# Shared projections of a two-layer decoder: a key or query pair's end in four parts with its scaling on ScalarE, tiles loaded a step ahead, and two pairs' forget gates moved to the front

## The chip, the core and the metric

The kernel runs on one core of a Trainium2 chip. A core has TensorE (matrix products; PE in the profile, PEld for its weight loads), VectorE (DVE), ScalarE (ACT), GpSimd (POOL), SyncE (SP, which issues the DMAs here) and 16 DMA engines. Each engine works through its own list of instructions in order and waits on semaphores for the others. The metric is the device time of one execution in microseconds (us).

## The reference, cut to what matters

One gated-DeltaNet layer (8 heads of 128) is followed by one forgetting-attention layer that reads a shared K/V. The change touches mainly the part between them: the projections to keys, queries, values, output gates and forget gates, all of the normalised residual stream `h` (2048 x 1024, float32).

```python
def shared_kv(h, kv_norm, kv_w, kv_forget_bias, kv_k_norm):
    u = rms_norm(h, kv_norm)
    k, v, f = jnp.split(u @ kv_w, [FOX_WIDTH, 2 * FOX_WIDTH], axis=-1)
    k = rms_norm(k.reshape(B, L, FOX_HEADS, HEAD_DIM), kv_k_norm)   # per head of 128
    log_f = jax.nn.log_sigmoid(f + kv_forget_bias)
    c = jnp.cumsum(log_f, axis=1)
    return k, v, c

def fox_mixer(h, k, v, c, w_in, q_norm, w_out):
    q, z = jnp.split(h @ w_in, [FOX_WIDTH], axis=-1)
    q = rms_norm(q.reshape(B, L, FOX_HEADS, HEAD_DIM), q_norm)
    o = fox_attention(q, k, v, c) * jax.nn.silu(z)
    return o @ w_out
```

## The kernel before, in words

The program has four stages: the DeltaNet layer (projections, chunked rule), its output product (class `Wout`), the shared projections (class `Shared`), and attention with its output product. Every product of two float32 matrices is done as three products of rounded halves (`split` writes a high and a low part, `mm3` adds three matmuls).

`Shared` takes the 2048 rows as 8 pairs of 128-row tiles, in three blocks of 2, 3 and 3 pairs (`BLOCKS`). For each block it runs through 8 groups of weight columns, two for each of the kinds k, q, v and z. In a group each 2x2 block product is done in seven products instead of eight (`PRODUCTS`, in the order P1 P6 P7 P5 P2 P4 P3), so a group is seven steps, and a step has 12 matmuls of 128x256 for each pair of the block: 3 pairs make 7*3*12 = 252 matmuls, 2 pairs 168. One pair's 12 matmuls are called a pair-step here.

What feeds and empties them:

- `raw` loads a group's weights (`w`), `sums` (POOL, line 913) forms `T1` to `T3` of the next group and `T4` of this one, `columns` splits them into `gh` (ACT cast, line 124) and `gl` (DVE subtraction, line 125), two products ahead, in three buffers. So a `gh` of a product waits until the product three before it is finished.
- `prep` makes the row operands `hP`, `lP` of a pair: it loads two tiles `ht` of `h_d`, scales them, transposes them on TensorE into `pth` and splits seven combinations. It is a generator; `run` takes its steps at fixed groups of the block before, and for the first block the loop at the end of `tile_yoco` takes them at the places in `ready` while `Wout` runs.
- The results `X` and `Y` of the products are gathered into `cc` by ACT (lines 984, 986) and DVE (line 989).
- `finish` ends a pair after its P3. For keys and queries: squares of the whole `cc` (ACT, line 1035), row sums by head `kss` (DVE, 1037 and 1038), root `krs` (POOL power, line 119), `cc` times `krs` (DVE, line 1041), and then, as two entries of `pend`, two `turn`s: four transposes into `ptr` (TensorE, line 1049), a scaled copy `kt` (ACT, line 1051) and a store. `tick` counts `pend` down once for each pair-step, so the first turn stands five pair-steps after the pair's P3 and the second six.
- `forget_weights` prepares the forget-gate columns `wf` and is called at the start of `run`; `forget` does a pair's gates (32 small matmuls into `pf`, a copy `fT`, two transposes) in the block's group 1.

```python
            ss = q2.tile([P, 8], F32, tag="kss", name="kss" + n)
            nc.vector.tensor_reduce(out=ss, in_=sq, axis=mybir.AxisListType.X, op=ALU.add)
            nc.vector.tensor_scalar(out=ss, in0=ss, scalar1=1.0 / P, scalar2=EPS, op0=ALU.mult, op1=ALU.add)
            rs = q2.tile([P, 8], F32, tag="krs", name="krs" + n)
            rsqrt(k, rs, ss, 8)
            nc.vector.tensor_tensor(out=c8, in0=c8, in1=rs.unsqueeze(2).to_broadcast([P, 8, P]), op=ALU.mult)
```

A scheduler of the language places each engine's instructions by priority and its own estimates, so the order on an engine can differ from the order in which the code names the operations; the orders shown further down are those of the built programs.

In the DeltaNet stage `gain` scales the weights of the shared projections ahead of time: at every third weight tile it loads a tile `wgr`, scales it on ACT (line 205) and stores it to `wg_d`.

## Time and profile before

| | |
|---|---|
| median of three runs | 3067.0 us (3064.26 to 3077.52) |
| the profiled execution | 3070.3 us, of which the program's span is 3068.3 us |
| DeltaNet stage, span 0 to 1186 us | 1186 us |
| rest of `Wout`, 1186 to 1414 us | 228 us |
| shared projections, 1414 to 2318 us | 904 us |
| attention and output, 2318 to 3068 us | 750 us |

Times inside the execution are counted from the span's start. In a row of a timeline stand the start, the duration, the engine, the line, the operation, the tile written and those read, and in brackets how long the engine had been idle before it and what ended that wait. Matmuls overlap, so 12 of 0.28 us that follow one another take about 1.4 us. A `PEclk` of 1.00 means TensorE at its higher level (2.4 GHz) throughout the stretch, 0.50 at its lower level (1.2 GHz).

### The profile page before, as it was taken

The numbers are of one execution on the slowest core, as the hardware profiler recorded it, in microseconds if no ns is written. First come the engines' busy times: TensorE is split into PE (matmuls) and PEld (weight loads), VectorE is DVE, ScalarE is ACT, GpSimd is POOL, SyncE is SP. The second block draws the span as 40 slices with busy tenths as digits, with TensorE's granted clock in tenths as the row PEclk, the third lists the DMA queues.
The fourth block names the chain that finished last, engine by engine and source line by source line (L and its number), as shares of the span: only waits on it lengthen the run. The fifth ranks groups of instructions, "written<-read, shape, count | busy, mean of one in ns | idle before, by whom it ended". The sixth has DMA issues, their size and how long they took to land.

```text
span 3068.3 us, 49714 instructions
## 1 busy us (share of the span) xinstructions
PE 2810.4 (92%) x17910; PEld 2434.8 (79%) x17910; DVE 2051.3 (67%) x5094; ACT 1448.2 (47%) x3288; POOL 991.8 (32%) x810
## 2 busy tenths in 40 slices
PE   7889999999999999988788988988897999999999
PEld 6677778877878787777788888978896888888787
DVE  6777766776777776445668555765557888888522
ACT  5445554454455444343444333433334776776421
POOL 6543111121111111244445233433322444444222
PEclk9999999999999999998888889989898999999999
DMA  6655764475457445343233223322224233332443
GB/s 225 216 183 175 227 192 148 146 252 185 146 176 243 143 135 160 115 153 126 96 124 124 76 80 111 126 76 76 93 95 127 89 94 94 103 94 86 138 144 107
DMA packets 296796, 421.86 MB, mean 137 GB/s; under 512 B 69739, under 2 KB 184678, under 8 KB 295526
## 3 DMA queue, kind: packets, MB, share of 16 engines
q1 hardware_dynamic: 296384, 418.63, 42.1%
q8 instruction: 141, 2.31, 0.3%
q14 instruction: 105, 0.86, 0.1%
q10 hardware_dynamic: 166, 0.06, 0.0%
HBM read 296.92 MB, written 121.70 MB: 136 GB/s over the span
## 4 chain that ended last, share of the span: by engine, by line
PE 52%; DVE 20%; POOL 5%; issue 5%; ACT 4%; DMA 3%; SPq 0%; DVEq 0%; POOLq 0%; ACTq 0%
PE Y L978 9%; PE X L978 5%; DVE acc_q L409 4%; PE pt L1312 3%; POOL krs L119 2%; DVE cc L1041 2%; PE ps L132 2%; PE ppwf L132 2%; PE ppwf L130 2%; PE ppwf L131 2%; PE ps L130 2%; PE ps L131 2%; PE po L132 2%; PE po L131 2%; PE po L130 2%
## 5 line engine op out<-in xcount | busy, mean ns | idle before, releaser
L130 PE MATMUL pp_q<-xh_q,wh_q 128*128 128x512 f32 x768 | 326.8, 425 | 1.5 <-ACT acc_q L407 0.8
L978 PE MATMUL Y<-gh_P,hP 128*128 128x256 f32 x1024 | 302.4, 295 | 14.3 <-DVE cc L989 11.3
L132 PE MATMUL pp_q<-xh_q,wl_q 128*128 128x512 f32 x768 | 308.4, 402 | 0.0
L131 PE MATMUL pp_q<-xl_q,wh_q 128*128 128x512 f32 x768 | 306.4, 399 | 0.0
L978 PE MATMUL Y<-gl_P,hP 128*128 128x256 f32 x1024 | 299.0, 292 | 0.0
L978 PE MATMUL Y<-gh_P,lP 128*128 128x256 f32 x1024 | 297.5, 291 | 0.0
L978 PE MATMUL X<-gh_P,hP 128*128 128x256 f32 x768 | 229.1, 299 | 19.8 <-POOL hrs L119 6.5
L913 POOL TENSOR_TENSOR T<-w,T 128x1024 f32<-128x1024 f32 x48 | 115.1, 2399 | 390.8 <-DVE gl_P L125 380.6
L409 DVE SCALAR_TENSOR_TENSOR acc_q<-cx_q,cols,acc_q 128x512 f32<-128x512 f32 x288 | 226.9, 788 | 13.6 <-ACT acc_q L407 10.5
L978 PE MATMUL X<-gl_P,hP 128*128 128x256 f32 x768 | 225.2, 293 | 8.9 <-DVE gl_P L125 8.9
L978 PE MATMUL X<-gh_P,lP 128*128 128x256 f32 x768 | 225.8, 294 | 2.1 <-DVE lP L125 2.1
L978 PEld LDWEIGHTS Y<-gh_P,hP 128*128 128x128 f32 x1024 | 206.8, 202 | 16.7 <-issue 9.3
L125 DVE TENSOR_TENSOR pl<-pt,ph 128x512 fp32r<-128x512 f32 (+1 forms) x320 | 191.5, 605 | 39.1 <-ACT ph L124 37.3
L124 ACT CAST ph<-pt 128x512 fp32r<-128x512 f32 (+1 forms) x320 | 161.5, 518 | 92.6 <-PE pt L1312 91.7
L978 PEld LDWEIGHTS Y<-gl_P,hP 128*128 128x128 f32 x1024 | 204.8, 200 | 0.0
L978 PEld LDWEIGHTS Y<-gh_P,lP 128*128 128x128 f32 x1024 | 204.5, 200 | 0.0
L1298 ACT ACTIVATE s<-s,nm 128x128 f32<-128x128 f32 (+15 forms) x128 | 154.3, 1206 | 65.9 <-DVE nm L1296 65.7
L412 ACT ACTIVATE th_q<-acc_q 128x512 f32<-128x512 f32 x96 | 60.6, 631 | 251.8 <-DVE acc_q L409 248.5
L1312 PE MATMUL pt<-ident,s 128*128 128x128 f32 x1088 | 172.7, 274 | 2.4 <-DVE pl L125 2.3
L989 DVE TENSOR_TENSOR cc<-cc,Y 128x256 f32<-128x256 f32 x256 | 104.9, 417 | 103.2 <-PE Y L978 102.7
L132 PEld LDWEIGHTS pp_q<-xh_q,wl_q 128*128 128x128 f32 x768 | 146.0, 190 | 34.2
L978 PEld LDWEIGHTS X<-gh_P,hP 128*128 128x128 f32 x768 | 155.9, 203 | 21.2 <-ACT gh_P L124 7.5
(485 smaller groups left out, 8369.3 us busy)
## 6 DMA issues: line engine op xcount, KB each, us to landing
w<-wg_d SPq DMA_DIRECT2D x48, 1024.0 KB, 5.0
wh_q<-w_d SPq DMA_DIRECT2D x72, 512.0 KB, 4.4
wl_q<-w_d SPq DMA_DIRECT2D x72, 512.0 KB, 4.4
wg_d<-wgr SPq DMA_DIRECT2D x32, 512.0 KB, 5.0
w_d<-wh_q SPq DMA_DIRECT2D x24, 512.0 KB, 4.7
w_d<-wl_q SPq DMA_DIRECT2D x24, 512.0 KB, 3.1
wh_q_z<-w_d SPq DMA_DIRECT2D x24, 512.0 KB, 3.5
wl_q_z<-w_d SPq DMA_DIRECT2D x24, 512.0 KB, 4.9
```

What stands on the lines that cost most here:

```text
L119: k.nc.gpsimd.tensor_tensor(out=out, in0=x, in1=k.mhalf[:, :n], op=ALU.pow)
L124: i = k.nc.scalar.copy(hi, src)
L125: (eng or k.nc.vector).tensor_tensor(out=lo, in0=src, in1=f(hi), op=ALU.subtract)
L130: nc.tensor.matmul(out, ah, bh, start=start, stop=False)
L131: nc.tensor.matmul(out, ah, bl, start=False, stop=False)
L132: nc.tensor.matmul(out, al, bh, start=False, stop=stop)
L409: nc.vector.scalar_tensor_tensor(out=acc, in0=cx[:, j:j + TB], scalar=cw[j], in1=acc, op0=ALU.mult, op1=ALU.add)
L913: self.k.nc.gpsimd.tensor_tensor(out=t, in0=a, in1=b, op=ALU.subtract)
L978: nc.tensor.matmul(R, a[:, kt], w[:, kt], start=first and kt + j == 0, stop=last and kt + j == 5, skip_group_check=True)
L989: nc.vector.tensor_tensor(out=dst, in0=src, in1=R, op=ALU.add)
L1298: e = nc.scalar.activation(s[:, 0:w], s[:, 0:w], AF.Exp, bias=nm, accum_out=ls[:, ii:ii + 1])
L1312: nc.tensor.transpose(out=pt[:, ii * P:(ii + 1) * P], in_=Ps[ii][:, j * P:(j + 1) * P], identity=k.ident)
```

## The change

1. A key or query pair's end is cut in four (`squares(0)` in `finish`, `root` one pair-step later, `norm` three after that, the turns one pair-step later than before). The squares and row sums come in two halves of 512 columns. The multiplication by `krs` goes from one DVE instruction of 128x1024 to eight ACT instructions of 128x128, each with its column of `krs` as scale. `cc` has five buffers instead of four, `kss` and `krs` four.
2. The gate kind z is done in two halves too.
3. `prep` loads a tile `ht` one step before its use, and `run` and `ready` step it accordingly (one step more per pair).
4. `forget_weights` is called before `prep` of the first block, with its tiles in other pools; the first block's `forget` runs ahead of all groups, the other blocks' as before.
5. `gain` scales and stores a tile at the call after its load.

```diff
@@ gain
+        if count[0] % 3 == 1 and loaded:
+            i, kt, wr, col = loaded.pop(0)
+            nc.scalar.activation(wr, wr, AF.Copy, scale=k.cols[:, col + kt:col + kt + 1])
+            nc.sync.dma_start(wg_d[i, kt], wr)
...
         nc.sync.dma_start(wr, w[kt * P:(kt + 1) * P, base:base + D])
-        nc.scalar.activation(wr, wr, AF.Copy, scale=k.cols[:, col + kt:col + kt + 1])
-        nc.sync.dma_start(wg_d[i, kt], wr)
+        loaded.append((i, kt, wr, col))
@@ Shared.prep
+        ht = load(2 * p)
+        yield
         for i in range(2):
             tt = 2 * p + i
-            ht = p2.tile([P, D], F32, tag="ht", bufs=1, name=f"ht{tt}")
-            nc.sync.dma_start(ht, h_d[tt * P:(tt + 1) * P, :])
...
                 nc.scalar.copy(q[i, kg], pt)
+                if (i, kg) == (0, 1):
+                    ht = load(2 * p + 1)
                 yield
@@ Shared.run
-        self.forget_weights()
+        gates = [self.forget(*pair) for pair in self.BLOCKS[0]]
+        for x in gates + gates:
+            next(x, None)
...
-                    cc[p] = q2.tile([P, 2, 512], F32, tag="cc", bufs=4, name=f"cc{nm}")
+                    cc[p] = q2.tile([P, 2, 512], F32, tag="cc", bufs=5, name=f"cc{nm}")
...
-            if gi in (1, 3) and pi in (0, 2, 4) and pi // 2 < len(pairs) and gi == 1:
+            if b and gi == 1 and pi in (0, 2, 4):
@@ Shared.finish
-            sq = self.q1.tile([P, 8, P], F32, tag="sq", name="sq" + n)
-            nc.scalar.activation(sq, c8, AF.Square)
-            ss = q2.tile([P, 8], F32, tag="kss", name="kss" + n)
-            nc.vector.tensor_reduce(out=ss, in_=sq, axis=mybir.AxisListType.X, op=ALU.add)
-            nc.vector.tensor_scalar(out=ss, in0=ss, scalar1=1.0 / P, scalar2=EPS, op0=ALU.mult, op1=ALU.add)
-            rs = q2.tile([P, 8], F32, tag="krs", name="krs" + n)
-            rsqrt(k, rs, ss, 8)
-            nc.vector.tensor_tensor(out=c8, in0=c8, in1=rs.unsqueeze(2).to_broadcast([P, 8, P]), op=ALU.mult)
+            def squares(hf):
+                sq = self.q1.tile([P, 4, P], F32, tag="sq", name=f"sq{n}_{hf}")
+                nc.scalar.activation(sq, c8[:, 4 * hf:4 * hf + 4], AF.Square)
+                nc.vector.tensor_reduce(out=ss[:, 4 * hf:4 * hf + 4], in_=sq, axis=mybir.AxisListType.X, op=ALU.add)
+
+            def root():
+                squares(1)
+                nc.vector.tensor_scalar(out=ss, in0=ss, scalar1=1.0 / P, scalar2=EPS, op0=ALU.mult, op1=ALU.add)
+                rsqrt(k, rs, ss, 8)
+
+            def norm():
+                for i in range(8):
+                    nc.scalar.activation(c8[:, i], c8[:, i], AF.Copy, scale=rs[:, i:i + 1])
+
+            squares(0)
+            pend.append([1, root])
+            pend.append([4, norm])
...
-            pend.append([5, lambda: turn(0)])
-            pend.append([6, lambda: turn(1)])
+            pend.append([6, lambda: turn(0)])
+            pend.append([7, lambda: turn(1)])
@@ tile_yoco
     sh = Shared(k, ins, dram, wg_d, sa)
+    sh.forget_weights()
...
-    ready = ready[0:4] + [ready[3] + 8 + 2 * i for i in range(7)] + ready[4:8] + [ready[7] + 8 + 2 * i for i in range(7)]
+    ready = [r for i in (0, 4) for r in [ready[i + 2] - 6] + [ready[i + 2] + 4 * j for j in range(4)]
+             + [ready[i + 2] + 24 + 2 * j for j in range(7)]]
```

ACT at the end of group 10 (a query group of the block with pairs 2, 3 and 4), before. In a name the first number is the group, the next the pair: `sq10_2` is that of pair 2; `gh11_P7` is the cast for product P7 of group 11.

```order
L1035 ACTIVATE sq10_2_19141<-cc10_2_18861 128x1024
L124 CAST gh11_P7_19196<-T11_3_19079 128x1024
L1035 ACTIVATE sq10_3_19162<-cc10_3_18891 128x1024
L984 COPY one11_2_19201<-X11_2_19200 128x256
L984 COPY one11_3_19216<-X11_3_19215 128x256
L984 COPY one11_4_19231<-X11_4_19230 128x256
L1035 ACTIVATE sq10_4_19183<-cc10_4_18921 128x1024
L1051 ACTIVATE kt10_2_0_19250<-ptr10_2_0_19245,qns_98 128x512
L124 CAST gh11_P5_19253<-T11_1_18943 128x1024
L1051 ACTIVATE kt10_2_1_19276<-ptr10_2_1_19271,qns_98 128x512
```

The same place after the change, from the copy `one11_2` to the first copy `kt` (both halves of the first pair's squares and `gh11_P7` stand ahead of it):

```order
L998 COPY one11_2_19354<-X11_2_19353 128x256
L998 COPY one11_3_19374<-X11_3_19373 128x256
L1053 ACTIVATE sq10_4_0_19336<-cc10_4_19057 128x512
L1063 ACTIVATE cc10_2_18997<-cc10_2_18997,krs10_2_19294 128x128 x3
L1053 ACTIVATE sq10_3_1_19339<-cc10_3_19027 128x512
L1063 ACTIVATE cc10_2_18997<-cc10_2_18997,krs10_2_19294 128x128 x3
L1053 ACTIVATE sq10_4_1_19368<-cc10_4_19057 128x512
L1063 ACTIVATE cc10_2_18997<-cc10_2_18997,krs10_2_19294 128x128 x2
L998 COPY one11_4_19397<-X11_4_19396 128x256
L1063 ACTIVATE cc10_3_19027<-cc10_3_19027,krs10_3_19312 128x128 x8
L124 CAST gh11_P5_19419<-T11_1_19087 128x1024
L1077 ACTIVATE kt10_2_0_19442<-ptr10_2_0_19437,qns_98 128x512
```

Between the squares of pairs 3 and 4 now stand the scalings of pair 2, so these squares come behind `krs10_2`; the casts of group 11 from P5 on and the first copy `kt` come behind the scalings of pair 3.

POOL at the same place, before (`T12_3` is the sum T3 of group 12):

```order
L913 TENSOR_TENSOR T11_2_19034<-w11_1_18797,T11_1_18943 128x1024
L913 TENSOR_TENSOR T11_2_19034<-w11_1_18797,T11_2_19034 128x1024
L119 TENSOR_TENSOR krs10_2_19146<-kss10_2_19143,mhalf_76 128x8
L913 TENSOR_TENSOR T12_3_19475<-w12_1_19193,w12_0_19191 128x1024
L119 TENSOR_TENSOR krs10_3_19167<-kss10_3_19164,mhalf_76 128x8
L119 TENSOR_TENSOR krs10_4_19188<-kss10_4_19185,mhalf_76 128x8
L913 TENSOR_TENSOR T12_1_19339<-w12_0_19191 128x1024
```

POOL there after the change:

```order
L925 TENSOR_TENSOR T11_2_19186<-w11_1_18920,T11_2_19186 128x1024
L925 TENSOR_TENSOR T12_3_19657<-w12_1_19346,w12_0_19344 128x1024
L119 TENSOR_TENSOR krs10_2_19294<-kss10_2_19293,mhalf_76 128x8
L119 TENSOR_TENSOR krs10_3_19312<-kss10_3_19311,mhalf_76 128x8
L119 TENSOR_TENSOR krs10_4_19335<-kss10_4_19334,mhalf_76 128x8
L925 TENSOR_TENSOR T12_1_19513<-w12_0_19344 128x1024
L925 TENSOR_TENSOR T12_2_19612<-w12_1_19346,T12_1_19513 128x1024
```

The sum `T12_3` of the next group has moved from behind the first pair's root to ahead of it. On TensorE, at this end of group 10, the transposes `ptr` of all three pairs stood within P6 of group 11 (the last one behind the first matmul of P7); after the change those of the first pair stand within P6, behind 6 pair-steps, those of the second in P7 and those of the third in P5.

TensorE at the start of the shared projections, before (`ppwg_15` is the last product of `Wout`, `X0_0` the first of pair 0):

```order
L130 MATMUL ppwg_15_1_15445<-wgwh7_13653,ohwg_15_15440 128x512
L131 MATMUL ppwg_15_1_15445<-wgwl7_13654,ohwg_15_15440 128x512
L132 MATMUL ppwg_15_1_15445<-wgwh7_13653,olwg_15_15441 128x512
L823 MATMUL pth4_0_15888<-ident_60,ht4_15885 128x128 x4
L978 MATMUL X0_0_15610<-gh0_P1_15576,hP1_0_14688 128x256
L978 MATMUL X0_1_15625<-gh0_P1_15576,hP1_1_14818 128x256
L978 MATMUL X0_0_15610<-gl0_P1_15577,hP1_0_14688 128x256
L978 MATMUL X0_0_15610<-gh0_P1_15576,lP1_0_14689 128x256
```

And after the change (`pf0`, `pf1` are the gates of pairs 0 and 1, 32 matmuls each):

```order
L131 MATMUL ppwg_15_1_15462<-wgwl7_13654,ohwg_15_15457 128x512
L132 MATMUL ppwg_15_1_15462<-wgwh7_13653,olwg_15_15458 128x512
L897 MATMUL pf0_15601<-hP1_0_14708,wf_14637 128x128
L897 MATMUL pf0_15601<-lP1_0_14709,wf_14637 128x128
...
L897 MATMUL pf1_15636<-hP4_1_14914,wf_14637 128x128
L897 MATMUL pf1_15636<-lP4_1_14915,wf_14637 128x128
L904 MATMUL pg0_15671<-ident_60,fT0_15634 128x32 x2
L992 MATMUL X0_0_15692<-gh0_P1_15593,hP1_0_14708 128x256
L992 MATMUL X0_0_15692<-gl0_P1_15594,hP1_0_14708 128x256
L904 MATMUL pg1_15677<-ident_60,fT1_15669 128x32 x2
```

The 64 gate matmuls stand ahead of the first product, and the transposes `pth4` of pair 2 are gone from this place.

## Rows read from the trace of the kernel before

**Rows 1.** The page: span of the profiled execution.

```profile
span 3068.3 us, 49714 instructions
```

**Rows 2.** Shared projections: busy us (xinstructions) of PE, PEld, DVE, ACT, POOL; PEclk; DMA.

```profile
1414.30:2318.00 903.70, 776.59 (x6005) 763.03 (x6003) 562.68 (x722) 344.59 (x484) 347.79 (x158) 0.91 0.29 99
```

**Rows 3.** The same by group: 2 pairs, 3 pairs, 3 pairs of kind v.

```profile
1503.20:1533.30 30.10, 24.59 (x185) 24.08 (x184) 19.08 (x23) 13.08 (x17) 13.80 (x7) 0.89 0.30 105
...
1806.90:1851.40 44.50, 36.94 (x278) 36.38 (x277) 25.79 (x31) 16.11 (x22) 16.02 (x8) 0.88 0.25 84
...
1900.00:1929.50 29.50, 29.27 (x249) 29.10 (x248) 14.41 (x21) 10.80 (x17) 11.61 (x6) 1.00 0.47 161
```

**Rows 4.** Waits of TensorE, 1420 to 2318 us: us, times, longest.

```profile
PE ptr L1049 <- DVE cc L1041: 61.6, 23, 4.5
...
PE ptr L1049 <- DVE kss L1038: 9.8, 4, 3.4
...
PE pth L823 <- DVE fT L888: 5.7, 1, 5.7
```

**Rows 5.** Timeline at the end of group 10: DVE.

```profile
1802.56 1.22 DVE L1037 TENSOR_REDUCE kss<-sq 128x8 f32<-128x1024 f32 x1 [0.61 <-ACT sq L1035]
...
1804.10 1.22 DVE L125 TENSOR_TENSOR gl_P<-T,gh_P 128x1024 fp32r<-128x1024 f32 x1
1806.85 3.36 DVE L1041 TENSOR_TENSOR cc<-cc,krs 128x1024 f32<-128x1024 f32 x1 [1.53 <-POOL krs L119]
```

**Rows 6.** The same stretch: ACT.

```profile
1801.47 1.06 ACT L1035 ACTIVATE sq<-cc 128x1024 f32<-128x1024 f32 x1 [1.68 <-DVE cc L989]
1802.95 1.05 ACT L124 CAST gh_P<-T 128x1024 fp32r<-128x1024 f32 x1 [0.42 <-PE Y L978]
```

**Rows 7.** The same stretch: POOL.

```profile
1804.27 2.54 POOL L119 TENSOR_TENSOR krs<-kss,mhalf 128x8 f32<-128x8 f32 x1 [0.74 <-DVE kss L1038]
1806.78 2.34 POOL L913 TENSOR_TENSOR T<-w,w 128x1024 f32<-128x1024 f32 x1
1811.62 1.64 POOL L119 TENSOR_TENSOR krs<-kss,mhalf 128x8 f32<-128x8 f32 x1 [2.50 <-DVE kss L1038]
```

**Rows 8.** The same stretch: transposes on TensorE.

```profile
1810.35 0.89 PE L1049 MATMUL ptr<-ident,cc 128*128 128x128 f32 x4 [3.18 <-DVE cc L1041]
...
1816.54 0.60 PE L1049 MATMUL ptr<-ident,cc 128*128 128x128 f32 x4
...
1822.20 1.09 PE L1049 MATMUL ptr<-ident,cc 128*128 128x128 f32 x4 [4.12 <-DVE cc L1041]
```

**Rows 9.** Line 1041: times, then ns (least/median/most).

```profile
L1041 DVE TENSOR_TENSOR cc<-cc,krs x32: 1224/3352/3366, 1461.7 to 2198.1; 128x1024 f32<-128x1024 f32 x32
```

**Rows 10.** Timeline: four scalings of 128x128 by a column on ACT.

```profile
646.03 1.14 ACT L431 ACTIVATE kd_q<-pt_q,eg_q 128x128 f32<-128x128 f32 x4 [0.59 <-PE pa_q1g L583]
```

**Rows 11.** Timeline, start of the shared projections: POOL and DVE.

```profile
1426.69 2.34 POOL L913 TENSOR_TENSOR T<-w,T 128x1024 f32<-128x1024 f32 x1 [0.38 <-DMA w<-wg_d]
1427.09 5.08 DVE L869 TENSOR_SCALAR wfz<-wfz,cols 128x8 f32<-128x8 f32 x8 [4.68 <-DMA wfz<-in_kv_w_dram]
...
1432.31 1.22 DVE L125 TENSOR_TENSOR gl_P<-T,gh_P 128x1024 fp32r<-128x1024 f32 x1
```

**Rows 12.** The same stretch: TensorE.

```profile
1421.24 0.77 PE L978 MATMUL X<-gh_P,hP 128*128 128x256 f32 x2 [6.55 <-POOL hrs L119]
...
1430.16 0.58 PE L978 MATMUL X<-gh_P,hP 128*128 128x256 f32 x1 [3.77 <-ACT gh_P L124]
```

**Rows 13.** Timeline of TensorE: transposes of the first block's rows.

```profile
1309.22 1.94 PE L823 MATMUL pth<-ident,ht 128*128 128x128 f32 x8 [4.99 <-issue]
...
1325.62 1.70 PE L823 MATMUL pth<-ident,ht 128*128 128x128 f32 x8 [3.87 <-DVE ht L818]
```

**Rows 14.** Line 205: what ACT waited for before it (us, times).

```profile
  DMA wgr<-in_kv_w_dram: 8.6, 4
  DMA wgr<-in_fox_w_in_dram: 6.0, 4
```

More of the change, by code (lines that the diff above doesn't have):

```diff
@@ L813, in prep, with load @@
         q = {}
+        def load(tt):
+            ht = p2.tile([P, D], F32, tag="ht", bufs=1, name=f"ht{tt}")
+            nc.sync.dma_start(ht, h_d[tt * P:(tt + 1) * P, :])
+            return ht
+        ht = load(2 * p)
+        yield
         for i in range(2):
             tt = 2 * p + i
-            ht = p2.tile([P, D], F32, tag="ht", bufs=1, name=f"ht{tt}")
-            nc.sync.dma_start(ht, h_d[tt * P:(tt + 1) * P, :])
             nc.vector.tensor_scalar(out=ht, in0=ht, scalar1=k.hrs[:, tt:tt + 1], scalar2=None, op0=ALU.mult)
@@ L861, in forget_weights @@
         nc = k.nc
-        self.wf = self.q1.tile([P, 12, P], F32R, name="wf")
-        wz = self.q2.tile([P, 2, 512], F32, tag="cc", bufs=4, name="wfz")
-        nc.gpsimd.memset(wz[:, 0, 0:P], 0.0)
-        nc.gpsimd.tensor_copy(self.wf, wz[:, 0, 0:P].unsqueeze(1).to_broadcast([P, 12, P]))
+        self.wf = self.p1.tile([P, 12, P], F32R, name="wf")
+        wz = self.p2.tile([P, 4, P], F32, tag="s1", name="wfz")
+        nc.gpsimd.memset(wz[:, 0], 0.0)
+        nc.gpsimd.tensor_copy(self.wf, wz[:, 0].unsqueeze(1).to_broadcast([P, 12, P]))
         wr = wz[:, 1, 0:12 * H].rearrange("p (t h) -> p t h", h=H)
@@ L998, in run @@
                         later = [self.prep(*nxt[0], h_d)]
-                    if gi == 1:
-                        next(later[0], None)
-                    if gi == 2:
+                    if gi in (1, 2):
                         next(later[0], None)
@@ L1007, in run @@
                     later = [self.prep(p, s, h_d) for p, s in soon]
-                if gi in (5, 6) and pi < 4:
+                if gi in (5, 6) and pi < 5:
                     next(later[gi - 5])
@@ L1012, in run @@
                         next(x, None)
+                    if pi == 4 and len(later) > 2:
+                        next(later[2])
                     if pi == 6 and len(later) > 2:
@@ L1033, in finish @@
             c8 = flat.rearrange("p (a d) -> p a d", d=P)
-            sq = self.q1.tile([P, 8, P], F32, tag="sq", name="sq" + n)
-            nc.scalar.activation(sq, c8, AF.Square)
-            ss = q2.tile([P, 8], F32, tag="kss", name="kss" + n)
-            nc.vector.tensor_reduce(out=ss, in_=sq, axis=mybir.AxisListType.X, op=ALU.add)
-            nc.vector.tensor_scalar(out=ss, in0=ss, scalar1=1.0 / P, scalar2=EPS, op0=ALU.mult, op1=ALU.add)
-            rs = q2.tile([P, 8], F32, tag="krs", name="krs" + n)
-            rsqrt(k, rs, ss, 8)
-            nc.vector.tensor_tensor(out=c8, in0=c8, in1=rs.unsqueeze(2).to_broadcast([P, 8, P]), op=ALU.mult)
+            ss = q2.tile([P, 8], F32, tag="kss", bufs=4, name="kss" + n)
+            rs = q2.tile([P, 8], F32, tag="krs", bufs=4, name="krs" + n)
+            def squares(hf):
[12 more added lines that the diff above has]
+            pend.append([4, norm])
             gain = k.cols[:, C_KN:C_KN + 1] if kind == "k" else k.qns
@@ L1054, in turn @@
                 nc.sync.dma_start(dst[h0:h0 + 2, :, p * 256:p * 256 + 256].rearrange("h p t -> p h t"), kt_)
-            pend.append([5, lambda: turn(0)])
-            pend.append([6, lambda: turn(1)])
+            pend.append([6, lambda: turn(0)])
+            pend.append([7, lambda: turn(1)])
             return
         if kind == "z":
-            th = self.q1.tile([P, 8, P], F32, tag="sq", name="th" + n).rearrange("p a d -> p (a d)")
-            nc.scalar.activation(th, flat, AF.Tanh, scale=0.5)
-            nc.vector.scalar_tensor_tensor(out=flat, in0=th, scalar=1.0, in1=flat, op0=ALU.add, op1=ALU.mult)
+            for t in range(2):
+                th = self.q1.tile([P, 4, P], F32, tag="sq", name=f"th{n}_{t}").rearrange("p a d -> p (a d)")
+                nc.scalar.activation(th, c[:, t], AF.Tanh, scale=0.5)
+                nc.vector.scalar_tensor_tensor(out=c[:, t], in0=th, scalar=1.0, in1=c[:, t], op0=ALU.add, op1=ALU.mult)
         dst = self.v if kind == "v" else self.z
```

5 lines of the change are left out of this document (3 added, 2 removed).

## Prediction, made before the changed kernel ran

> **What bounds the kernel now.** I read the page first, then busy time by stage, then by group of weight columns, then what TensorE waited for, and last a timeline of one group's end. The span is 3068.3 us [rows 1]; the profiled execution took 3070.3 us, 3.3 above the median of 3067.0. TensorE is the engine that is nearly always busy, and it has the most slack to lose in the shared projections: of 903.7 us it is busy 776.6, and its granted clock is 0.91 [rows 2], so 18% of the stage (163 us) ran at the lower of the two levels (1.2 instead of 2.4 GHz).
>
> Groups of three pairs show where. A value group does 249 matmuls in 29.5 us at clock 1.00, 0.1185 us each [rows 3]. A query group has 252 of them (29.9 us) and 24 transposes at 0.15 (four in 0.60 us, [rows 8]), 3.6 us: 33.5 us of work. It took 44.5 at clock 0.88 [rows 3]. Of the excess of 11.0 us, 7.3 are two waits ahead of transposes, 3.18 and 4.12 us [rows 8]; the rest is the lower clock that follows them (0.88 is 24% of 44.5, 10.7 us at half rate). A group of two pairs has 168*0.1185 + 16*0.15 = 22.3 us of work and took 30.1: excess 7.8 [rows 3]. There are 8 groups of three pairs and 4 of two that end in transposes (32 pairs), so 8*11.0 + 4*7.8 = 119 us is all that a better pair end can give. The list of waits says the same: `ptr` waited 61.6 + 9.8 us [rows 4].
>
> The chain behind the first wait: square 1801.47 to 1802.53 [rows 6], sum 1802.56 to 1803.78 [rows 5], root 1804.27 to 1806.81 [rows 7], product with `krs` 1806.85 to 1810.21 [rows 5], transposes at 1810.35. TensorE had been there since 1810.35 - 3.18 = 1807.17 [rows 8].
>
> **1. The pair's end (three pairs).** Of 32 products with `krs` the least took 1.22 us and the median 3.35 [rows 9]; the long ones start while POOL works on a `T` (1806.78 to 1809.12, [rows 7]) and end 1.1 us after it, so they were held up by it. The change takes them off VectorE. On ACT a pair needs eight scalings; four took 1.14 us [rows 10], so one follows the other by 0.25 and eight take 2.1. That row reads PSUM, where the new ones read and write SBUF; from below the free VectorE product, 1.22, and from above eight separate ones, 3.1 (0.39 each: 1.14 less three steps of 0.25), bound it. I take 2.1, the nearest row. The half squares I take as 0.53 (half of 1.06), the half sums as 0.61.
>
> New chain for the first pair, in the order on ACT that the rows of the change show, with clock times of this trace: its half square at 1801.47, to 2.00; pair 3's, to 2.6; the cast of P7, held by TensorE until 1802.95, to 1804.0 [rows 6]; the second half square to 1804.55. On DVE `gl` of P7 ends at 1805.32 [rows 5], the second half sum at 1805.9, `kss` at 1806.1. On POOL the root now stands behind `T12_3`, which waits for that same `gl`: 1805.3 to 1807.65. Root at 1.64 us [rows 7]: to 1809.3. Then three scalings, a half square of pair 3, three scalings, after which the first turn's four blocks are ready: 1809.3 + 6*0.25 + 0.53 + 0.15 = 1811.5. TensorE comes to this turn one pair-step (12*0.1185 = 1.42 us) later than before, at 1808.6. It waits 2.9 us, hardly less than the 3.18 it waited.
>
> The second wait, 4.12 us, goes. The turns of the second pair stand in P7 and those of the third in P5 of the next group, 8 and 9 pair-steps behind their P3; the second pair's scalings end by 1815.7 (second half sum 1811.6, root 1813.5, eight scalings), and TensorE, after its 2.9 us, comes there at about 1817.5. What is late next: the copies `kt` stand behind eight scalings on ACT and `ptr` has two buffers, worth some 0.5 us. Queued behind the waiting scalings are the casts from P5 on; the cast of P5 follows the second pair's scalings at 1815.7, its `gl` is done by 1818, and P5 is due at about 1820. That cover is 2 us.
>
> After: work 33.5, wait 2.9, buffers 0.5, lower clock after a single wait 2.9/7.3 of 3.7 = 1.5: 38.4. Gain 6.1 per group, 8 groups: 49 us. Bounds: if the root comes before `T12_3` or that sum is early, the first wait is 0.6 (gain 9.5, 76 us); if the roots take 2.54 us and the scalings 3.1, it is 4.8 (gain 3.3, 26 us).
>
> One page speaks against this part. The Trainium skill's "ScalarE: Activation LUTs", section "Rules for kernel authors", sends a multiplication to VectorE, and its section "What ACT_TABLE_LOAD costs" gives 186 ns plus 93 for a column operand plus 0.833 per element, with 93 ns of overlap: as an estimate 0.29 us from one to the next and 2.4 us for eight. By that the first wait grows by 0.3 us and the gain falls by some 3 us over the kernel; the row of this trace (0.25) decides.
>
> **2. The pair's end (two pairs).** Here `T1` of the next group also stands ahead of the roots on POOL, and it needs the `gl` of P5. From the end of the first pair's P3: P1 of both pairs is done at 4.25 us, the copies `one` at 4.65, cast and `gl` of P5 at 7.0, `T1` at 9.4, the root, sharing with a `gl`, at 11.9 (2.54 in rows 7), the first scaling at 12.3. TensorE comes there after 6 pair-steps and 5 matmuls, 9.1: wait 3.2. With 0.5 for buffers and 1.5 for the clock: 22.3 + 5.2 = 27.5 instead of 30.1. Gain 2.6, 4 groups: 10 us (bounds -4 to 25).
>
> **3. Gates of two pairs first.** TensorE idled 6.55 us ahead of the first product [rows 12]; 64 gate matmuls, taken at the same 0.1185 as the others (7.6 us), now fill that. In group 1 they cost 7.6 us and the transposes of the next pair's rows a wait of 5.7 [rows 4]: 13.3 saved. At the start the preparation of `wf` sat in DVE's queue, 1427.09 to 1432.2, of which 4.68 waiting for a DMA [rows 11], and `gl` of P6 came behind it at 1432.31; without it, behind `T2` (1429.03) and its cast, it comes at 1430.2: 2.1 us. But the first product, which ran in the open at 1421.24, starts about 1 us later behind the gates. Sum 14 us (bounds 5 to 20).
>
> **4. Loads a step ahead.** TensorE waited 4.99 and 3.87 us for the first block's rows [rows 13]. The first load still stands behind the same store on SP's queue, and the transposes only 5 matmuls later on TensorE (1.1 us): at most 1 saved. The second pair's stand 13 later (twice as wide as those above: 13*2*0.1185 = 3.1 us): 3 saved, with a little clock 4.5 together (0 to 9). The later blocks' `ht` loads, five buffers of `cc` and the halves of z: nothing; there VectorE's splits of rows are the limit, and they stay. In `gain`, ACT waited 8.6 + 6.0 us [rows 14], an engine half idle there: 1 us.
>
> **Sum.** 49 + 10 + 14 + 4.5 + 1 = 78.5 off 3070.3 is 2991.8; less the 3.3 to the median: **2988 us**.
>
> **Rivals.**
> - *The waits go altogether* (the sums on POOL run earlier than I place them, the halves overlap better). For: the sum waits in DVE's queue, which gets 3.36 us per pair emptier. Against: `T12_3` needs the same `gl` as before. All 119 us go, with 14 and 5: 2929. Chance 0.17.
> - *The root is the new tail*: POOL's sum ahead of it comes late (its weights, or a `gl` behind ACT), the first wait grows to 6 us and what is queued on ACT behind it leaves a second of 2. Excess per group 11.0 - 2, none gained with two pairs: 16 + 14 + 4.5: 3032. Chance 0.14.
> - *ACT becomes the bound and the kernel slower*: all work behind a scaling waits with it. If eight scalings take 3.1 us and each root 2.54, three pairs add 3.0 + 2.7 us to ACT's queue ahead of the cast of P5, against 2 us of cover; P5 starts 3.7 late on top of a wait of 4.8, with the clock excess 12. It decides from a further 2 us per group on (another sum between two roots, 2.34): excess 15, 8*4 + 4*3 = 44 lost against 19 gained: 3092. Against: ACT is busy 16.1 of 44.5 us [rows 3]. Chance 0.07.
>
> **How the numbers follow.** My forecast has 0.62, with a range of its own from 2960 to 3012. The range for 8 in 10 reaches into both neighbours: 2940 to 3036. A measurement here tells about 0.5% (15 us) from no change. Faster by more: the forecast, the first rival, and most of the second: 0.88. Within: 0.05. Slower: 0.07.
>
> **What would show it.** Right: waits of `ptr` fall from 71 us to about 40, all by ACT's scalings and at a pair's first turn alone; a three-pair query group takes 38 us, a value group 29.5; 64 gate matmuls follow the last `Wout` product; the product on DVE is gone. Step 1 is wrong if a second wait per group stays, or if TensorE waits for casts of P5 or P2 instead; step 2 if `T1` runs before the squares; step 3 if the wait ahead of P6 is still near 4 us. The forecast fails as a whole if the granted clock of the stage stays at 0.91.

## The result and the profile after

The changed kernel took 3021.1 us (3016.5 to 3028.1, 4 runs) against 3070.2 of the kernel before on the same chip: ratio 0.984, interval 0.981 to 0.987. It gained 49 us where 79 were forecast (2988, from the 3067.0 of the first three runs). The runs that follow come from several chips, so they are compared by their ratio to the kernel before on the same chip. The profiled execution took 3023.7 us. Its span:

```profile
span 3021.9 us, 50002 instructions
```

The stretches that answer to [rows 2, 3]: the shared projections from the first gate matmul on; two pairs, from TensorE's wait for the first transposes in group 2 to that in group 3; three pairs of kind q, from that wait in group 11 to that in group 12; and 29.5 us in group 13, of kind v (us; busy us of PE, PEld, DVE, ACT, POOL; PEclk; DMA).

```profile
1419.50:2270.40 850.90, 747.52 (x6006) 735.72 (x6004) 519.12 (x725) 420.44 (x784) 337.35 (x156) 0.94 0.31 105
1502.70:1532.70 30.00, 24.02 (x185) 23.82 (x184) 20.53 (x29) 18.15 (x36) 13.91 (x6) 0.89 0.34 106
1796.40:1833.30 36.90, 33.20 (x278) 32.43 (x277) 20.35 (x32) 23.09 (x49) 14.46 (x8) 1.00 0.30 101
1870.00:1899.50 29.50, 28.57 (x243) 28.39 (x243) 15.97 (x23) 10.07 (x15) 11.28 (x6) 1.00 0.37 121
```

The three-pair query group fell from 44.5 to 36.9 us and its granted clock rose from 0.88 to 1.00; the clock of the whole stage rose from 0.91 to 0.94. Two pairs, from wait to wait, stand at 30.0, as before (30.1); but group 2 from its first matmul to that of group 3 has grown from 30.4 to 35.2 us. The stretch of kind v is 29.5 us long by choice, here as in [rows 3]: the whole of group 13 takes 32.7 us (32.0 before). TensorE's waits, which answer to [rows 4] (us, times, longest):

```profile
PE ptr L1075 <- ACT cc L1063: 43.1, 17, 6.1
...
PE pth L833 <- DVE ht L828: 13.1, 6, 5.4
PE pg L904 <- DVE fT L900: 11.0, 2, 9.5
...
PE X L992 <- ACT one L998: 7.7, 4, 2.5
PE pth L833 <- issue: 7.3, 1, 7.3
PE ptr L1075 <- ACT kt L1077: 6.7, 4, 5.1
```

Transposes of pairs wait 49.8 us instead of 71.4 (for the gates' copy `fT`, ahead of a turn, they wait 5.0 more, 3.6 before). New are 11.0 us for the gates and 7.7 for the copies `one`, and the waits for scaled rows (`pth`) have doubled from 9.1 to 20.4.

The whole difference, by stretches of one profile each (us). A group runs from its first matmul to that of the next. The column `Wout` runs from the last product of `At` with `R`, near the end of the DeltaNet rule, to the last product of `Wout`; the rule runs beside `Wout`, past the 1186 us at which the table of before parts the stages. "Start" ends where group 2 begins, so it holds groups 0 and 1.

| kernel | `Wout` | start | groups 2-4 (2 pairs) | 5-8 | eight k/q groups of 3 pairs | 13-16 |
|---|---|---|---|---|---|---|
| before | 130.9 | 83.7 | 91.7 | 112.2 | 380.2 | 144.9 |
| changed | 135.4 | 70.7 | 94.1 | 115.6 | 332.2 | 147.6 |
| E1 pair's end alone | 133.1 | 83.3 | 86.4 | 109.9 | 333.2 | 145.0 |
| E2 all but the pair's end | 135.4 | 74.5 | 96.7 | 113.9 | 378.7 | 148.1 |
| E3 scaling on VectorE | 135.2 | 73.8 | 92.0 | 112.6 | 350.6 | 147.4 |
| E4 loads as before | 136.8 | 71.0 | 91.1 | 110.2 | 332.6 | 146.5 |
| E5 gate weights between pairs | 132.3 | 72.0 | 91.3 | 112.7 | 332.0 | 147.1 |
| E6 `gain` as before | 135.6 | 71.5 | 93.2 | 115.9 | 332.9 | 147.6 |
| E7 E1, two square buffers | 132.7 | 84.5 | 83.4 | 109.7 | 325.3 | 145.1 |
| E8 E1, scaling order | 131.6 | 83.1 | 85.6 | 112.8 | 328.5 | 144.5 |
| E9 E7 and scaling order | 133.1 | 82.9 | 83.5 | 112.1 | 323.2 | 144.0 |
| E10 E9 and gates first | 130.7 | 75.0 | 87.4 | 110.4 | 321.7 | 144.1 |
| E11 E10 and rows spread | 131.2 | 72.9 | 86.2 | 109.8 | 321.8 | 145.2 |
| E12 E11, gates turned later | 131.2 | 70.7 | 87.0 | 110.0 | 320.2 | 144.2 |

Of what is left out, groups 21 to 23 differ by under 1 us, attention and output took 749.1 to 753.7 us, and that last product of the DeltaNet rule stood at 1276.6 to 1290.2 us; so a median of four or five runs says little below some 6 us, and the stretches say more. They have a spread of their own, though: seven of the kernels (the changed one, E1, E3 to E6 and E8) have the same single wait of 3.3 us in group 8, and it took them 33.3 to 35.9 us, so 2 to 3 us in one column of one profile show nothing by themselves.

### The end of group 10 and of a two-pair group, after

ACT at the end of group 10 (columns as in [rows 5]):

```profile
1798.00 0.99 ACT L1063 ACTIVATE cc<-cc,krs 128x128 f32<-128x128 f32 x3 [2.99 <-POOL krs L119]
1798.89 0.61 ACT L1053 ACTIVATE sq<-cc 128x512 f32<-128x512 f32 x1
1799.41 0.97 ACT L1063 ACTIVATE cc<-cc,krs 128x128 f32<-128x128 f32 x3
...
1802.38 2.45 ACT L1063 ACTIVATE cc<-cc,krs 128x128 f32<-128x128 f32 x8 [0.64 <-POOL krs L119]
1804.74 1.03 ACT L124 CAST gh_P<-T 128x1024 fp32r<-128x1024 f32 x1
```

The transposes of the same pairs on TensorE:

```profile
1798.45 0.33 PE L1075 MATMUL ptr<-ident,cc 128*128 128x128 f32 x1 [1.77 <-ACT cc L1063]
1800.14 0.44 PE L1075 MATMUL ptr<-ident,cc 128*128 128x128 f32 x2 [1.36 <-ACT cc L1063]
...
1806.41 0.66 PE L1075 MATMUL ptr<-ident,cc 128*128 128x128 f32 x4 [0.57 <-ACT kt L1077]
```

The first wait is 1.77 + 1.36 = 3.1 us, in two parts, where 2.9 was worked out, the wait for buffers 0.57 against 0.5, and the second wait of 4.12 us [rows 8] is gone. Eight scalings take 2.45 us: 0.387 for one and 0.295 from one to the next, more than the 0.25 taken from [rows 10]. From the figures of the Trainium skill's "ScalarE: Activation LUTs", section "What ACT_TABLE_LOAD costs", the prediction had estimated 0.29, and this trace agrees with it.

POOL and DVE just before. The small DVE operation is the scale of the row sums, 128x8, which the root waits for:

```profile
1793.82 2.40 POOL L925 TENSOR_TENSOR T<-w,w 128x1024 f32<-128x1024 f32 x1 [2.23 <-DVE gl_P L125]
1796.33 1.64 POOL L119 TENSOR_TENSOR krs<-kss,mhalf 128x8 f32<-128x8 f32 x1
```

```profile
1794.38 1.87 DVE L1058 TENSOR_SCALAR kss<-kss 128x8 f32<-128x8 f32 x1
...
1800.47 0.17 DVE L1058 TENSOR_SCALAR kss<-kss 128x8 f32<-128x8 f32 x1
```

The root does come behind `T12_3`, as forecast, but not only in POOL's order: the operation that feeds it took 1.87 instead of 0.17 us and ended with that sum.

A two-pair key end, group 1 in group 2, first ACT, then TensorE:

```profile
1498.30 0.63 ACT L1053 ACTIVATE sq<-cc 128x512 f32<-128x512 f32 x1 [1.89 <-DVE kss L1054]
...
1503.98 0.63 ACT L1053 ACTIVATE sq<-cc 128x512 f32<-128x512 f32 x1 [1.78 <-DVE kss L1054]
1508.46 4.79 ACT L1063 ACTIVATE cc<-cc,krs 128x128 f32<-128x128 f32 x16 [3.85 <-POOL krs L119]
```

```profile
1495.41 0.39 PE L992 MATMUL X<-gh_P,hP 128*128 128x256 f32 x1 [2.53 <-ACT one L998]
1499.24 0.39 PE L992 MATMUL X<-gh_P,hP 128*128 128x256 f32 x1 [2.17 <-ACT one L998]
1508.92 0.47 PE L1075 MATMUL ptr<-ident,cc 128*128 128x128 f32 x1 [5.98 <-ACT cc L1063]
```

Half squares have one buffer and wait for the sum of the half before. Copies `one` stand behind them in ACT's queue, and TensorE waits for these, which was in no term of the forecast. The wait for the scaling is 5.98 us where 3.2 was worked out.

### The profile page after: what moved, and what is told of

Read it like the earlier page. It is cut to its first block, busy times and chain, and to the rows that moved or that the text cites. A ratio compares the mean times of both kernels' runs of the same rounds, so it can differ in the third digit from the quotient of the medians.

```text
span 3021.9 us, 50002 instructions
## 1 busy us (share of the span) xinstructions
PE 2785.3 (92%) x17910; PEld 2410.1 (80%) x17910; DVE 2010.1 (67%) x5110; ACT 1526.1 (51%) x3592; POOL 985.7 (33%) x810
## 4 chain that ended last, share of the span: by engine, by line
PE 55%; DVE 18%; ACT 6%; issue 4%; POOL 4%; DMA 3%; SPq 0%; DVEq 0%; POOLq 0%; ACTq 0%
PE Y L992 9%; PE X L992 6%; PE pt L1339 4%; DVE acc_q L413 3%; PE ps L132 2%; PE ppwf L130 2%; PE ppwf L132 2%; PE ppwf L131 2%; PE ps L130 2%; PE ps L131 2%; PE po L132 2%; PE po L131 2%; PE po L130 2%; PE ppwg L131 1%; PE ppwg L132 1%
## 5 line engine op out<-in xcount | busy, mean ns | idle before, releaser
L1003 DVE TENSOR_TENSOR cc<-cc,Y 128x256 f32<-128x256 f32 x256 | 105.4, 417 | 113.9 <-PE Y L992 112.4
L132 PEld LDWEIGHTS pp_q<-xh_q,wl_q 128*128 128x128 f32 x768 | 145.7, 190 | 34.3
L125 DVE TENSOR_TENSOR gl_P<-T,gh_P 128x1024 fp32r<-128x1024 f32 x96 | 129.8, 1353 | 62.6 <-ACT gh_P L124 58.7
```

The costliest lines, as they stand in the source:

```text
L125: (eng or k.nc.vector).tensor_tensor(out=lo, in0=src, in1=f(hi), op=ALU.subtract)
L132: nc.tensor.matmul(out, al, bh, start=False, stop=stop)
L1003: nc.vector.tensor_tensor(out=dst, in0=src, in1=R, op=ALU.add)
```

## The experiments

**E1. The pair's end alone.** The kernel before with `finish` of the changed one, and five buffers for `cc`:

```diff
-            nc.vector.tensor_tensor(out=c8, in0=c8, in1=rs.unsqueeze(2).to_broadcast([P, 8, P]), op=ALU.mult)
...
+            squares(0)
+            pend.append([1, root])
+            pend.append([4, norm])
```

> The kernel before with the pair's end in four parts, the five buffers of cc and the halves of z; loads, gates and the weights' scaling stay as before. Theory (the pair's end gives all that was gained, and it gives it in the groups of three pairs alone): a three-pair query group takes 37 to 38 us (before 44.5), a two-pair group that ends in transposes 29 to 31 us (before 30.1), 'Wout' ends at 1414 us, and the time is 3022 to 3027 us. Rival (the gain needs the freed places of the other edits, above all the loads a step ahead): three-pair query groups stay above 41 us and the time at 3040 us or more.

Measured: 3013.0 us (ratio 0.983, 0.981 to 0.985), as much gained as by the whole change (0.984, 0.981 to 0.987) or more. The eight three-pair groups take 333.2 us, 47.0 less, and groups 2 to 4 take 5.3 less. So the gain is this part's; it needs none of the others, and the rival falls. That it gives something with two pairs too was not expected by the theory, and the time is 9 us below its bounds.

**E2. Everything but the pair's end.**

```diff
-            pend.append([1, root])
-            pend.append([4, norm])
...
+            nc.vector.tensor_tensor(out=c8, in0=c8, in1=rs.unsqueeze(2).to_broadcast([P, 8, P]), op=ALU.mult)
```

> The changed kernel with the pair's end and kind z as before (one square, one sum, one product on VectorE, turns after five and six pair-steps, four buffers of cc). Theory: three-pair query groups are back at 44 to 45 us; gates first save about 13 us in groups 0 and 1, the row operands lose 4 to 5 us at the end of 'Wout' and some 5 us in the changes of block, so 3060 to 3068 us. Rival (gates and loads are worth the 18 us that were forecast, and the pair's end hides them): 3050 us.

Measured: 3075.7 us, ratio 1.003 (1.001 to 1.004): loads, gates and `gain` together are worth nothing or a little less, outside both expectations on the slow side. The start gains 9.2 us; `Wout` gives back 4.5, groups 2 to 4 5.0, and 13 to 16 3.2.

**E3. The scaling back on VectorE, at its new place.**

```diff
-                for i in range(8):
-                    nc.scalar.activation(c8[:, i], c8[:, i], AF.Copy, scale=rs[:, i:i + 1])
+                nc.vector.tensor_tensor(out=c8, in0=c8, in1=rs.unsqueeze(2).to_broadcast([P, 8, P]), op=ALU.mult)
```

> The changed kernel with 'norm' as one VectorE product of 128x1024, as before, at its new place three pair-steps after the root. Theory (the product on VectorE was held up by the sums on POOL, so taking it off VectorE matters): the product takes 2.4 to 3.4 us in most groups, three-pair query groups take 40 us or more, 3035 to 3050 us. Rival (the gain comes from the halves and the later turns; which engine scales is nothing): query groups within 1 us of the changed kernel's 37 us, 3015 to 3026 us.

Measured: 3039.8 us (0.990 to 0.994), a query group 39.6 us. The time is the theory's, its reason is not: the product took 1224 to 1227 ns in all 32 cases, since the root on POOL now ends behind the sum: none of the 32 ran beside a sum on POOL, where 18 of the 32 products of [rows 9] did, and those 18 took 3.35 us or a little more. Line 1062 of this kernel (ns: least/median/most), then DVE and ACT at the end of group 10:

```profile
L1062 DVE TENSOR_TENSOR cc<-cc,krs x32: 1224/1224/1227, 1476.5 to 2176.6; 128x1024 f32<-128x1024 f32 x32
...
1804.60 1.23 DVE L1062 TENSOR_TENSOR cc<-cc,krs 128x1024 f32<-128x1024 f32 x1 [1.75 <-POOL krs L119]
1805.74 0.68 DVE L1054 TENSOR_REDUCE kss<-sq 128x4 f32<-128x512 f32 x1
...
1806.46 0.64 ACT L1053 ACTIVATE sq<-cc 128x512 f32<-128x512 f32 x1 [3.28 <-DVE kss L1054]
```

The product waits for its root at the head of DVE's queue, the sums of the next pair stand behind it, and the half square behind those on ACT waits 3.28 us. So of the 48.0 us, 29.6 came with halves and later turns (380.2 to 350.6) and 18.4 with the engine. That the engine helps by keeping DVE's queue moving is what these rows suggest; no run tests it by itself.

**E4. Loads and steps of the row operands as before.**

```diff
-                if (i, kg) == (0, 1):
-                    ht = load(2 * p + 1)
...
-                if gi in (5, 6) and pi < 5:
+                if gi in (5, 6) and pi < 4:
```

> The changed kernel with the loads of the row tiles and the steps of the row operands as before. Theory (the new steps put the transposes of rows where VectorE has not yet scaled the tile): the waits for scaled rows fall from 20 us to about 11, 'Wout' ends 1 to 2 us earlier, the last groups of a block are 1 to 2 us shorter each, 3014 to 3018 us. Rival (loads a step ahead save what was forecast, 4.5 us): 3024 to 3027 us.

Measured: 3015.1 us, inside the theory's bounds, but by the ratio (0.983, 0.981 to 0.985) not told apart from the changed kernel. Nor is it where the theory said: `Wout` is 1.4 us longer, groups 2 to 8 are 8.4 shorter (3.0 and 5.4), and the waits for scaled rows fall to 16.0 us, not to 11. The profiles of all kernels sort out what belongs to the edit. Group 7 took 32.0 to 32.6 us in the five with the new steps and 29.4 to 30.1 in the nine with the old ones, groups 13 and 14 32.7 or 32.8 against 31.8 to 32.1, and group 2, where the gates stand first and the rows of pair 2 are not spread, 34.3 to 36.2 against 32.2 and 32.5. That is some 6 us. The other 2.5 of groups 5 to 8 are group 8, which differs as much between kernels with the same steps. The loads a step ahead helped where 4.5 us were forecast, by a third of that, and cost more in the groups, where the forecast had nothing. Even that third is gone when the gate weights stand between the row pairs: `Wout` takes 132.3 us with the new loads (E5) and 130.7 to 131.2 with the old ones (E10 to E12).

**E5. Gate weights prepared between the first and second row pair.**

```diff
-    sh.forget_weights()
...
+            if len(ready) == len(ALL) // 2:
+                sh.forget_weights()
```

> The changed kernel with forget_weights called between the steps of the first and the second row pair, within the 'Wout' stage, instead of ahead of both. Theory (its load and its scalings stood ahead of the first row tile in SP's and VectorE's queues): the first wait for rows falls from 7.3 us to about 5, the second from 5.4 to about 4, 'Wout' takes 131 to 132 us instead of 135.4, and the time is about 4 us less, 3015 to 3019 us. Rival (the steps of the loads cost this): 'Wout' stays at 135 us or more.

Measured: 3020.6 us (3012.6 to 3024.6), which tells nothing by itself; the stretch does. `Wout` takes 132.3 us, 3.1 less. What stood ahead of the first row tile in the changed kernel, DVE and then TensorE:

```profile
1308.71 1.17 DVE L881 TENSOR_SCALAR wfz<-wfz,cols 128x8 f32<-128x8 f32 x8 [2.99 <-issue]
...
1311.66 1.81 DVE L828 TENSOR_SCALAR ht<-ht,hrs 128x1024 f32<-128x1024 f32 x1
```

```profile
1313.57 1.94 PE L833 MATMUL pth<-ident,ht 128*128 128x128 f32 x8 [7.33 <-issue]
...
1333.48 1.94 PE L833 MATMUL pth<-ident,ht 128*128 128x128 f32 x8 [5.37 <-DVE ht L828]
```

And TensorE with the weights between the pairs:

```profile
1307.25 1.94 PE L833 MATMUL pth<-ident,ht 128*128 128x128 f32 x8 [5.28 <-issue]
...
1323.70 1.94 PE L833 MATMUL pth<-ident,ht 128*128 128x128 f32 x8 [3.62 <-ACT hP L124]
```

Both waits fall, from 7.33 to 5.28 and from 5.37 to 3.62, to about the values before [rows 13], and the rival falls.

**E6. `gain` as before.**

```diff
-        loaded.append((i, kt, wr, col))
+        nc.scalar.activation(wr, wr, AF.Copy, scale=k.cols[:, col + kt:col + kt + 1])
+        nc.sync.dma_start(wg_d[i, kt], wr)
```

> The changed kernel with 'gain' as before: scaled and stored at the call of the load. Theory A (the new order saves ScalarE waits but lengthens the DeltaNet stage, which in five profiles stood at 1283 to 1290 us with it and 1277 to 1283 without): 3 to 6 us less, 3012 to 3018 us. Theory B (the DeltaNet stage differs from run to run whatever 'gain' does): 3018 to 3024 us.

Measured: 3021.7 us, ratio 0.984 (0.982 to 0.987), the same as the changed kernel. Theory B: this edit does nothing that can be told. The last product of the DeltaNet rule stood at 1276.6 to 1284.7 us in the nine profiles with `gain` as before and at 1280.8 to 1290.2 in the five with it moved, 4 us later on average; so a small loss is not excluded.

**E7. E1 with two buffers for the half squares and four for `cc`.**

```diff
-                sq = self.q1.tile([P, 4, P], F32, tag="sq", name=f"sq{n}_{hf}")
+                sq = self.q1.tile([P, 4, P], F32, tag="sq", bufs=2, name=f"sq{n}_{hf}")
```

> The pair's end alone (as in the run of that name) with two buffers for the halves of the squares and four for cc, which the memory allows. Theory (in groups of two pairs the second half square waits for the sum of the first, and so the copies 'one' behind it on ScalarE come late; the roots come behind T1): groups 2 to 4 fall from 86.4 us to 80 to 84, three-pair groups by up to 1 us each; 3000 to 3010 us. Rival (VectorE's queue sets when the sums are done; a second buffer only makes the square wait elsewhere): 3011 to 3016 us.

Measured: 3005.6 us, ratio 0.979 (0.976 to 0.983), inside the theory's bounds; its slowest run is faster than E1's fastest. Groups 2 to 4 take 83.4, the eight others 325.3 (7.9 less). Its wait for scalings, against 39.7 in E1:

```profile
PE ptr L1061 <- ACT cc L1049: 24.9, 18, 2.8
```

No such wait is longer than 2.8 us now. In this build the scheduler also placed the first root ahead of `T1` in two-pair groups, so there the buffer and the order on POOL aren't told apart; with three pairs the order on POOL was the same in seven of the eight groups, so the gain there is the buffer's. It came with one buffer of `cc` fewer, so the fifth, which no run tests alone, is at least not needed for it.

**E8. E1 with the scalings in the order 0, 1, 4, 5, 2, 3, 6, 7.**

```diff
-                for i in range(8):
+                for i in (0, 1, 4, 5, 2, 3, 6, 7):
```

> The pair's end alone with the eight scalings in the order 0, 1, 4, 5, 2, 3, 6, 7, so that the first turn's four blocks are the first four. Theory (the first turn waits for the root and then for six scalings with a half square between; the new order leaves four): the first wait falls by 0.5 to 1.1 us, twelve groups, 3003 to 3009 us. Rival (the second turn then waits that much longer): 3011 to 3016 us.

Measured: 3011.0 us, within noise of E1. The eight groups gain 4.7 us, groups 5 to 8 lose 2.9 (2.5 of it in group 8, which no pair's end reaches): inconclusive by the time, and below what the theory said.

**E9. E7 and E8 together.** The two edits of E7 and E8.

> The pair's end alone, with two buffers for the half squares (four for cc) and the scalings in the order 0, 1, 4, 5, 2, 3, 6, 7. Theory (the two edits act on different waits, the square's buffer and the scalings behind the root): their gains add up, the eight three-pair groups that end in transposes take 320 to 323 us together and groups 2 to 4 take 82 to 83 us, 3000 to 3004 us. Rival (both shorten the same wait, which is nearly gone with the one): as with the two buffers alone, 325 us for the eight groups, 3004 to 3008 us.

Measured: 2997.7 us, ratio 0.978 (0.976 to 0.980), the eight groups 323.2, groups 2 to 4 83.5. Compared with E7 they gain 2.1 us, less than the 4.7 of the order alone, so the two gains do not add up; the rest of the difference in the medians is not in these stretches (the DeltaNet rule of its profile ended 6.2 us earlier). So the order is worth little once the buffer is there.

**E10. E9 with the gates first, their weights as in E5.**

```diff
+        gates = [self.forget(*pair) for pair in self.BLOCKS[0]]
+        for x in gates + gates:
+            next(x, None)
```

> As the run before, and the gates of the first two pairs ahead of all groups, their weights prepared between the two row pairs; loads and the scaling of weights as before. Theory (gates first save 12 us in groups 0 and 1, but the wait for gates in group 1 was cover for the row operands of pair 2, so group 2 gives 5 us back): group 2 takes 31 to 33 us instead of 27, 'Wout' stays at 131 to 133 us, 6 to 8 us less than the run before. Rival (with the second buffer group 2 loses nothing): 12 us less.

Measured: 2994.8 us, ratio 0.977 (0.975 to 0.979). The start gains 7.9 us, groups 2 to 4 give 3.9 back, group 2 alone 5.2 (27.0 to 32.2). The theory's place and its 5 us are there; the gain at the start is smaller than the 12 it said, and the total with it (2.8 us by the medians, with intervals that overlap).

**E11. E10 with the rows of pair 2 spread over groups 1 to 4.**

```diff
-                    if gi == 1:
-                        next(later[0], None)
-                    if gi == 2:
-                        next(later[0], None)
+                    if gi in (1, 2, 3, 4) and pi % 2 == 0:
+                        next(later[0], None)
```

> As the run before, with the row operands of pair 2 taken one step at every other product of groups 1 to 4 instead of at every product from group 1 on. Theory (in group 2 TensorE waits for copies 'one' and squares that stand behind the row splits on ScalarE and VectorE): group 2 falls to 28 us, groups 3 and 4 rise by up to 1 us each, 2 to 5 us less than the run before. Rival (the splits only move: groups 3 and 4 take what group 2 gives): no less than the run before.

Measured: 2992.3 us (2989.6 to 2993.6), ratio 0.976 (0.974 to 0.977). Group 2 falls to 30.0, not to 28, groups 3 and 4 take 1.0 more together, and the start falls by 2.1. Beside E10 the intervals overlap, so that the spreading helps is likely and not shown. A query group of three pairs in it, and its wait for scalings:

```profile
1772.40:1808.90 36.50, 34.61 (x278) 33.98 (x277) 19.36 (x33) 23.15 (x49) 14.38 (x8) 0.95 0.29 102
```

```profile
PE ptr L1062 <- ACT cc L1050: 21.2, 18, 3.0
```

**E12. E11 with the gates' transposes six pair-steps later.**

```diff
-        for x in gates + gates:
-            next(x, None)
+        for x in gates:
+            next(x)
+            pend.append([5, lambda x=x: next(x, None)])
```

> As the run before, but the transposes pg of the first two pairs' gates stand six pair-steps later, behind P7, instead of within the first product. Theory (the copy fT of the second pair stands behind the subtractions gl of P6 and P7 on VectorE, and the transposes that wait for it hold back 21 of the 24 matmuls of P1): the 9 to 10 us wait for fT goes, P1 runs at once and TensorE waits some 5 to 6 us for P6's columns instead, group 0 takes 29 to 30 us instead of 33.7, 2987 to 2990 us. Rival (P6's columns set the time and P1 fits anywhere): group 0 stays at 33 us or more, 2990 to 2994 us.

Measured: 2990.0 us (2984.3 to 2991.2), ratio 0.974 (0.973 to 0.975): the lowest here (the interval overlaps E11's), 79 us under the kernel before on the same chip. Group 0 stays at 33.6, as the rival said, and the time is between the two; the start gains 2.2 us, since the first product no longer waits for the first pair's `fT`. TensorE in group 0, then ACT:

```profile
1430.62 0.58 PE L982 MATMUL X<-gh_P,hP 128*128 128x256 f32 x1 [7.05 <-ACT one L988]
```

```profile
1426.95 1.04 ACT L124 CAST gh_P<-T 128x1024 fp32r<-128x1024 f32 x1 [7.66 <-POOL T L914]
1429.26 1.04 ACT L124 CAST gh_P<-T 128x1024 fp32r<-128x1024 f32 x1 [1.26 <-POOL T L914]
1430.21 0.64 ACT L988 COPY one<-X 128x256 f32<-128x256 f32 x2
```

The wait for `fT` is gone and another has its place: the copies `one` of P1 now stand on ACT behind the casts for P6 and P7, each of which waits for a sum on POOL. So the gates' transposes do not set group 0; these sums, with the order on ACT, do.

## Why the prediction was right, and where it was not

The mechanism was right and carries the result: TensorE waited at the pair's end, the clock fell after it, and the change takes about a third of both away (`ptr` waits 49.8 us instead of 71.4; by the clock, 12% of the stage at the lower level instead of 18%). The waits were to fall to about 40, all of them for scalings; 6.7 us are for the copies `kt`. The number was less right than the mechanism: 3021 lies outside the forecast's own range (2960 to 3012), nearer to the second rival's 3032 than to 2988, and inside the range for 8 in 10 because that reaches into the rivals. By the forecast's steps:

1. *Three pairs, 49 us.* Measured 48.0 (380.2 to 332.2). The chain came as drawn: a first wait of 3.1 us (2.9), none at the second place, 0.57 for buffers (0.5), though scalings took 2.45 instead of 2.1. But that the sum came within 1 us is in part luck. The group worked out gained 7.6 us, not 6.1, since it lost nothing to the clock (1.00; 1.5 us were allowed); other groups of the eight did, at clocks down to 0.91. And groups 9 and 17, in which the gates of a block stand too, gained only 4.4 and 3.9: there TensorE waits 5.10 us for a `kt` and 5.04 for `fT`, which the working did not look at.
2. *Two pairs, 10 us.* This step failed in the changed kernel: groups 2 to 4 lost 2.4 us. E1 shows that the pair's end alone gives 5.3 there, so three quarters of the error (7.7 of 10.2 us) is another: the forecast took these groups as if only the pair's end changed in them. E4 puts 3.0 us on the loads' steps (2.7 of it in group 2), and what remains to E1, 4.7 (91.1 less 86.4), comes by elimination with the gates first and lies in group 2 alone (27.8 to 32.5), as E10's 5.2 there bears out. The smaller part goes with the single buffer of the half squares, which the working passed over although the code shows one buffer for two halves: 3.0 us by E7, where the root's place on POOL changed too.
3. *Gates first, 14 us.* The start fell by 13.0, though it also holds the first two-pair end. The fill worked as forecast, and `gl` of P6 came earlier:

```profile
1434.88 2.27 DVE L125 TENSOR_TENSOR gl_P<-T,gh_P 128x1024 fp32r<-128x1024 f32 x1 [6.72 <-ACT gh_P L124]
...
1438.33 0.40 DVE L900 COPY fT<-pf 32x256 f32<-32x256 f32 x1
```

   It ends at 1437.15, 17.5 us after `Wout`'s last product (1419.7), against 19.2 before (1433.5 less 1414.3): 1.7 earlier where 2.1 was said. But the copy `fT` of the second pair stands behind this `gl` and the next, and the transposes `pg` wait 9.50 us for it (the row of `pg` above): the wait ahead of P6 has another name and stays, which is what the prediction had named as this step's failure. And two prices were missing: the weights' preparation in the row operands' queue (3.1 us, E5), and group 1, whose wait for gates had been time in which the rows of pair 2 were split. With the gates gone, group 2 has to pay (5.2 us in E10, of which spreading the rows in E11 takes back 2.2).
4. *Loads ahead, 4.5 us.* Wrong in sign, by the stretches; the ratio of E4 does not show it. The stretches of E4 are 7.4 us shorter without them (3.0, 5.4 and 1.1 in the groups, less 1.4 in `Wout`, 0.3 at the start and 0.4 in the others); without group 8, which differs by itself, that is 5. The saving at `Wout` was 1.4. What failed is the sentence that puts the later blocks' `ht` loads at nothing: group 7 loses some 2.5 us, group 2 2.7, groups 13 and 14 0.6 each.
5. *`gain`, 1 us.* Nothing that can be told (E6).

So of 78.5 us, 46.4 came in the profiles (3068.3 less 3021.9). The missing 32 are about 10 in groups 2 to 4 (7.8 forecast, 2.4 lost), 9 at `Wout` (4.5 forecast, 4.5 lost, of which 3.1 are the gate weights), 6 in groups 5 to 8 and 13 to 16 (some 2.5 of it group 8's own spread), 4 at the start (14 and the first pair's end, 2.6, against 13.0) and 3 in the rest.

The rivals: *the waits go altogether* fell (49.8 us stay). *The root is the new tail* is what happened with two pairs, a first wait of 6 us, and not with three; its mechanism on POOL was real, its price was taken too wide. Its time is nevertheless the nearest, since the two-pair groups and the loads lost what the three-pair groups did not. *ACT becomes the bound* did not come: the cast of P5 ran at 1804.74, right behind the scalings, and TensorE was not kept.

## What to carry to other kernels

When a waiting stage is also the time in which another engine prepares the next block, removing the wait moves that preparation under something else: look at what ran beside the wait before counting it as gained. An instruction that waits for a small result belongs on the engine whose queue holds the least behind it; its own duration matters less (1.22 us on VectorE lost to 2.45 on ScalarE here). A buffer that is cut in halves needs two of them, or the halves run one after the other (7.9 us in the eight groups of E7).
